# The low-part products of a flow-matching layer, moved behind the high-part products

## The chip, the cores and the metric

The kernel runs on one core of a Trainium2 chip. The metric is the device time of one execution in microseconds (us), as the median of several runs. Beside it there is a profile: one execution recorded by the hardware profiler.

## The reference, cut to what matters

One transformer-like layer is applied to 512 latent tokens and 128 context tokens, 640 in all, with a model width of 2048:

```python
h = _rmsnorm(x, norm1_g) * (1.0 + sc1) + sh1
p = h @ w_in                                  # 2048 x 5408
o_a, s_fin = _rwkv7_bidir(shift(p[..., :C_SHIFT]), s0, lp)
o_b = _chunk_gmlp(gelu(p[..., C_SHIFT:]), lp)
x = x + g1 * (concat([o_a, o_b]) @ w_out)     # 2048 x 2048
h = _rmsnorm(x, norm2_g) * (1.0 + sc2) + sh2
ff = (silu(h @ w_ffn_gate) * (h @ w_ffn_up)) @ w_ffn_down   # 2048 x 5632, 5632 x 2048
y = _rmsnorm(x + g2 * ff, final_norm_g)
```

The modulation vectors (`sh1`, `sc1`, ...) come from `silu(c) @ w_mod`. Everything is float32, and the large products have to keep nearly float32 accuracy.

## The kernel before, in words

**Split products.** TensorE multiplies in a faster, less exact format (fp32r). To keep the accuracy, each operand is split in two: `hi` is the value cast to fp32r, and `lo` is what the cast left over. A block of 128 x 128 weights and its activations then take three products into the same PSUM bank: `hi` weights by `hi` activations, `hi` weights by `lo` activations, and `lo` weights by `hi` activations. The fourth, `lo` by `lo`, is left out. A product here is one matmul of 128 x 128 weights with 320 columns (half of the tokens).

**Weight tiles.** Weights come in tiles of four such blocks (`[P, 4, P]`), in one transfer on the SyncE queue. For each tile ScalarE (ACT) casts `raw` to `hi`, then VectorE (DVE) subtracts `hi` from `raw` to make `lo`. In the FFN this is the helper `parts` (lines 1423 and 1424); for `w_in` and `w_out` it is `split` (lines 168 and 169). `raw`, `hi` and `lo` have three buffers each in the pool `st`, so the cast for a tile must wait until TensorE has read the `hi` of three tiles earlier, and the subtraction until it has read the `lo` of three tiles earlier.

**Stages.** In order of time:

- The modulation columns, the first norm and the product with `w_in`, block by block in `win` (lines 184 to 194): for each half of the tokens and each block `k`, the three products at lines 190, 191 and 192. After `k` = 1 and `k` = 3 the function `between` hands TensorE over to pieces of the RWKV preparation and the gMLP, which three queues of generators deal out.
- The RWKV recurrence, with the first half of the product with `w_out` dealt out between its hops.
- The second half of `w_out`: `four_blocks` (lines 1482 to 1484), one output block `m` after another, first for token half 0, then for half 1. `squares` squares each finished block on ACT and adds four of them up on GpSimd (POOL); `stats` (line 1462) sums over the partitions with a matmul by a matrix of ones. After the last group of a half it computes the norm factor `rs` with a DVE scaling, an ACT square root and a DVE reciprocal (lines 1465 to 1467). The normalised blocks of half 0 are made beside the blocks of half 1 (`first_half`, line 1392).
- The FFN. The first two output rows of gate and up are computed plainly (`plain`, lines 1571 to 1573). All others go through `seven` (lines 1642 to 1644), a Strassen-Winograd scheme with seven products where eight would be needed: 42 steps for gate and up (tiles of four blocks, two tiles a product) and 48 steps for the down projection (one tile a product). The 22 blocks of the down projection's inner dimension go in six chunks `CHK` = 3, 3, 4, 4, 4, 4, eight steps each; so in the first two chunks a tile has three blocks. Sums of weight tiles are made on POOL (`combined`, line 1552). The results of the products are taken from PSUM by hooks (`Gate`, `Sum` with lines 1876 to 1880, `Last`, `End`), written in the code some four products after the product itself. Near a change of chunk, new activation operands are split as well (`put_in`, lines 1708 on ACT and 1709 on DVE, three or four blocks at a time). In the last chunk, each PSUM bank is opened by a dummy matmul (line 2033) and filled with the sum so far by ACT (line 2034).

**What sets the order.** Each engine takes its instructions in a fixed order. On TensorE that order is the one written in the code in the set-up with the first three blocks of `w_in`, and in the recurrence (`manual_schedule`). In the other stages, and on the other engines, a planner that belongs to the framework arranges the instructions before the launch, by its own estimate of when each is ready, earlier code first. So the order on ACT, DVE and POOL isn't written out in the kernel and can come out another way when the program changes.

In a tile of `seven` the lines are these (`f` and `l` mark the first and the last product of a bank):

```python
for k in range(nk):
    xk = x(i, 4 * q + k)
    f, l = q == 0 and k == 0 and not filled, q == nq - 1 and k == nk - 1 and last
    TE.matmul(ps, hi[:, k, :], xk[:, 0, :], start=f, stop=False)
    TE.matmul(ps, hi[:, k, :], xk[:, 1, :], start=False, stop=False)
    TE.matmul(ps, lo[:, k, :], xk[:, 0, :], start=False, stop=l)
```

Of the kernel before, what the change touches and what calls it, by code (L numbers as in the profile page):

```python
# [21 lines left out]
KB = D // P  # L22
# [67 lines left out]
def flow_step(ctx: ExitStack, tc, x_prompt, x_sample, state_rwkv, c, c_ctx, w_mod, b_mod,  # L90
# [27 lines left out]
    for h in range(2):  # L118
        s = slice(CH * h, CH * h + CH)
# [64 lines left out]
    def win(halves, q, hi, lo, hfs=(0, 1), step=lambda k: None):  # L184

        for hf in hfs:
            s = slice(HALF * hf, HALF * hf + HALF)
            for k in range(4):
                kb = 4 * q + k
                TE.matmul(halves[hf], hi[:, k, :], h_hi[:, kb, s], start=(kb == 0), stop=False)  # L190
                TE.matmul(halves[hf], hi[:, k, :], h_lo[:, kb, s], start=False, stop=False)  # L191
                TE.matmul(halves[hf], lo[:, k, :], h_hi[:, kb, s], start=False, stop=(kb == KB - 1))  # L192
                wide[0] += 1
                step(k)

# [1165 lines left out]
    X = {}  # L1361
# [68 lines left out]
    with ExitStack() as ph:  # L1430
# [58 lines left out]
        for hf in range(2):  # L1489
            s = slice(HALF * hf, HALF * hf + HALF)  # L1490
            for m in range(KB):
                if hf or m >= AHEAD:
                    four_blocks(hf, m, 0)
                ps = four_blocks(hf, m, 1)
                if hf and m in (6, 7, 8, KB - 1):
                    for _ in range(2):
                        next(first)
                if sqs and (sqs[0][1] >= 12 or m % 4 == 1):
                    stats()
                add_out(m, [ps, ps], hf)  # L1500
                nc.sync.dma_start(d_x1[m][:, s], x1T[m][:, s])
                squares(hf, m)
                if hf and m > 1:
                    for kb in HALVES[m - 2:m - 1] if m < 14 else HALVES[2 * m - 16:2 * m - 14]:
                        first_half(kb)
                    if 4 <= m < 12:
                        j, i = divmod(m - 4, 2)
                        operand(1 + i, j, x1T[j + 8 * i][:, t1])
# [47 lines left out]
    def plain(e):  # L1556

        n, q, hs = PLAIN[e]
        for u in range(2):
            for b in range(2):  # L1560
                hi, lo = READY.pop(0) if READY else parts(PW.pop(0))
                next(loads, None)
                for h in hs:
                    if (n, u, h) not in CP:
                        CP[n, u, h] = pP.tile([P, 512], F32, tag="P", name="C")[:, 0:HALF]
                    ps, i = CP[n, u, h], ((1, 2), (5, 4))[h][b]
                    for k in range(4):
                        xk = X[i, 4 * q + k]
                        m = DONE.get((n, u, h), 0)
                        DONE[n, u, h] = m + 3  # L1570
                        TE.matmul(ps, hi[:, k, :], xk[:, 0, :], start=m == 0, stop=False)
                        TE.matmul(ps, hi[:, k, :], xk[:, 1, :], start=False, stop=False)
                        TE.matmul(ps, lo[:, k, :], xk[:, 0, :], start=False, stop=m == 45)

    def plain_out(n, h):

# [38 lines left out]
    def seven(b11, b12, b21, b22, x, hook, nk=4, bank=fresh, last=True, end=False):  # L1615

        def combine(out, a, b):
            combined(out, a, b, nk)
        t3 = [st.tile([P, 4, P], F32, tag="raw", name="t3", bufs=3) for _ in b11]
        combine(t3, b22, b12)  # L1620
        combine(b12, b12, b11)
        s6, s4 = b22, b21
        if end:
            s6, s4 = ([xap.tile([P, 4, P], F32, tag=next(wtags), name="rawd")] for _ in range(2))
            combine(s6, b22, b12)
            combine(s4, b21, s6)
        src = {1: b11, 2: b21, 3: b22, 7: t3, 5: b12, 6: s6, 4: s4}
        seq = PEND if end else PORD
        order = [raw for i in seq for raw in src[i]]

        ready = [parts(order.pop(0), nk)]
        for o, i in enumerate(seq):
            ps, filled = bank(i)
            nq = len(b11)
            for q in range(nq):
                hi, lo = ready.pop()
                if order:
                    ready.append(parts(order.pop(0), nk))
                for k in range(nk):
                    xk = x(i, 4 * q + k)  # L1640
                    f, l = q == 0 and k == 0 and not filled, q == nq - 1 and k == nk - 1 and last
                    TE.matmul(ps, hi[:, k, :], xk[:, 0, :], start=f, stop=False)  # L1642
                    TE.matmul(ps, hi[:, k, :], xk[:, 1, :], start=False, stop=False)  # L1643
                    TE.matmul(ps, lo[:, k, :], xk[:, 0, :], start=False, stop=l)  # L1644
            if i == 3 and not end:
                combine(b22, b22, b12)
                combine(b21, b21, b22)
            if last:
                hooks.append(lambda o=o, ps=ps: hook(o, ps))
            tick()  # L1650
            yield o
# [474 lines left out]
```

## Time and profile before

| | us |
|---|---|
| median of 3 runs | 3223.48 (3221.9 to 3225.47) |
| the profiled execution, its own time | 3213.3 |
| its span, first to last instruction | 3211.5 |
| TensorE busy by the page | 3088.0 (96%) |
| DVE busy | 2330.3 (73%) |
| ACT busy | 1460.1 (45%) |
| POOL busy | 1219.0 (38%) |

The profiled execution is one of its own, and 10.2 us below the median of the runs. The end of a matmul is modelled by the profiler and lies about 309 ns after its start, though the next one starts 147 ns after it; so "busy" on TensorE says that work was in flight, and a wait shows as idle only beyond those 309 ns. In the views, PE is TensorE's multiplying and PEld its loading of weights. A row of waits names who waited, for whom, and then microseconds in total, how many times, and the longest.

### The profile page before, as it was taken

The page shows a single profiled execution, that of the slowest core. Times are in us where ns is not written, and L with a number is a line of the kernel's source. Part 1 is how long each engine was busy: PE and PEld are TensorE (multiplying, and loading weights), DVE is VectorE, ACT ScalarE, POOL GpSimd, SP SyncE. Part 2 cuts the span into 40 slices and gives each one's busy share as a digit, 9 for nine tenths or more (in the row PEclk, how much of TensorE's full clock was granted, in tenths as well). Part 3 has the DMA queues.
Part 4 walks back from the last instruction along what each step waited for, and adds up shares of the span by engine and source line. Part 5 has one row for each costly group of instructions (what it writes and reads, how often), then busy time and mean ns, then how long its engine had stood idle before and what let it go on. Part 6 is the DMA issues. An engine that isn't in the chain of part 4 may idle for free.

```text
span 3211.5 us, 72260 instructions
## 1 busy us (share of the span) xinstructions
PE 3088.0 (96%) x28216; PEld 2858.2 (89%) x28216; DVE 2330.3 (73%) x4107; ACT 1460.1 (45%) x3197; POOL 1219.0 (38%) x1065
## 2 busy tenths in 40 slices
PE   6999989999999999999999999999999999999997
PEld 3688778788878888899999999999999999999997
DVE  4558666676657677767877777777777788887788
ACT  3344544454444444346644444444444454444365
POOL 2001121211122024311465566556655645555542
PEclk9999999999999999999999999999999999999999
DMA  9767786777778687564434434343344364553453
GB/s 372 239 187 203 210 215 171 209 218 193 201 198 216 210 275 253 173 200 133 141 116 130 127 105 123 118 124 118 113 128 126 104 199 152 159 165 112 140 165 122
DMA packets 740438, 550.88 MB, mean 172 GB/s; under 512 B 141056, under 2 KB 673504, under 8 KB 731264
## 3 DMA queue, kind: packets, MB, share of 16 engines
q1 hardware_dynamic: 727136, 532.47, 55.0%
q0 software_dynamic: 10624, 13.23, 1.9%
q8 instruction: 222, 3.64, 0.5%
q14 instruction: 120, 0.98, 0.1%
q10 hardware_dynamic: 2336, 0.57, 0.1%
HBM read 437.79 MB, written 110.95 MB: 171 GB/s over the span
## 4 chain that ended last, share of the span: by engine, by line
PE 56%; DVE 5%; issue 4%; DMA 3%; POOL 2%; ACT 2%; SPq 0%; DVEq 0%; POOLq 0%; ACTq 0%
PE P L1644 15%; PE P L1642 15%; PE P L1643 15%; DVE lo L1424 1%; PE big L1482 1%; PE big L1484 1%; PE big L1483 1%; PE big L1039 1%; PE big L190 1%; PE big L192 1%; PE big L191 1%; PE big L1041 1%; PE big L1040 1%; DMA opd<-d_op 1%; DMA rawd<-in_w_ffn_down_dram 1%
## 5 line engine op out<-in xcount | busy, mean ns | idle before, releaser
L1644 PE MATMUL P<-xo,lo 128*128 128x320 f32 x2352 | 727.1, 309 | 0.8 <-DVE lo L1424 0.7
L1642 PE MATMUL P<-xo,hi 128*128 128x320 f32 x2352 | 727.0, 309 | 0.7 <-ACT hi L1423 0.7
L1643 PE MATMUL P<-xo,hi 128*128 128x320 f32 x2352 | 726.9, 309 | 0.0
L1424 DVE TENSOR_TENSOR lo<-raw,hi 128x512 fp32r<-128x512 f32 x526 | 500.8, 955 | 174.4 <-ACT hi L1423 169.9
L1423 ACT CAST hi<-raw 128x512 fp32r<-128x512 f32 x526 | 326.7, 621 | 484.0 <-PE P L1643 392.1
L190 PE MATMUL big<-h_hi,hi 128*128 128x320 f32 x1376 | 447.3, 325 | 8.1 <-ACT hi L168 4.5
L1644 PEld LDWEIGHTS P<-xo,lo 128*128 128x128 f32 x2352 | 441.5, 188 | 1.8 <-DVE lo L1424 1.8
L1642 PEld LDWEIGHTS P<-xo,hi 128*128 128x128 f32 x2352 | 441.6, 188 | 1.0 <-ACT hi L1423 1.0
L1643 PEld LDWEIGHTS P<-xo,hi 128*128 128x128 f32 x2352 | 441.6, 188 | 0.0
L192 PE MATMUL big<-h_hi,lo 128*128 128x320 f32 x1376 | 431.1, 314 | 0.7 <-DVE lo L169 0.6
L191 PE MATMUL big<-h_lo,hi 128*128 128x320 f32 x1376 | 431.1, 313 | 0.7 <-DVE h_lo L352 0.4
L1552 POOL TENSOR_TENSOR raw<-raw 128x512 f32<-128x512 f32 x252 | 408.5, 1631 | 14.1 <-DVE lo L1424 2.7
L1644 PE MATMUL P<-xd,lo 128*128 128x320 f32 x1232 | 384.5, 312 | 16.3 <-DVE lo L1424 16.2
L1642 PE MATMUL P<-xd,hi 128*128 128x320 f32 x1232 | 382.7, 311 | 1.5 <-ACT hi L1423 0.3
L1643 PE MATMUL P<-xd,hi 128*128 128x320 f32 x1232 | 381.4, 310 | 0.0
L169 DVE TENSOR_TENSOR lo<-raw,hi 128x512 fp32r<-128x512 f32 x268 | 183.4, 689 | 200.6 <-ACT hi L168 185.1
L190 PEld LDWEIGHTS big<-h_hi,hi 128*128 128x128 f32 x1376 | 260.9, 190 | 58.1 <-issue 34.8
L1423 ACT CAST hi<-rawd 128x512 fp32r<-128x512 f32 (+1 forms) x288 | 168.8, 587 | 240.7 <-PE P L1643 203.1
L168 ACT CAST hi<-raw 128x512 fp32r<-128x512 f32 x268 | 164.5, 618 | 225.7 <-PE big L191 123.8
L191 PEld LDWEIGHTS big<-h_lo,hi 128*128 128x128 f32 x1376 | 261.3, 190 | 5.1 <-DVE h_lo L352 1.1
L192 PEld LDWEIGHTS big<-h_hi,lo 128*128 128x128 f32 x1376 | 260.3, 189 | 5.6 <-DVE lo L169 1.6
L1644 PEld LDWEIGHTS P<-xd,lo 128*128 128x128 f32 x1232 | 231.9, 188 | 23.2 <-DVE lo L1424 22.8
(404 smaller groups left out, 6052.8 us busy)
## 6 DMA issues: line engine op xcount, KB each, us to landing
wt<-in_w_mod_dram SPq DMA_DIRECT2D x96, 1024.0 KB
raw<-in_w_ffn_gate_dram SPq DMA_DIRECT2D x182, 256.0 KB
raw<-in_w_ffn_up_dram SPq DMA_DIRECT2D x182, 256.0 KB
rec<-d_S SPq DMA_DIRECT2D x80, 576.0 KB
raw<-in_w_in_dram SPq DMA_DIRECT2D x172, 256.0 KB
rawd<-in_w_ffn_down_dram SPq DMA_DIRECT2D x128, 256.0 KB
raw<-in_w_out_dram SPq DMA_DIRECT2D x96, 256.0 KB
xd<-d_os SPq DMA_DIRECT2D x66, 320.0 KB
```

Source lines behind the costliest of these rows:

```text
L168: S.copy(hi, raw)
L169: V.tensor_sub(lo, raw, hi.bitcast(F32))
L190: TE.matmul(halves[hf], hi[:, k, :], h_hi[:, kb, s], start=(kb == 0), stop=False)
L191: TE.matmul(halves[hf], hi[:, k, :], h_lo[:, kb, s], start=False, stop=False)
L192: TE.matmul(halves[hf], lo[:, k, :], h_hi[:, kb, s], start=False, stop=(kb == KB - 1))
L1039: TE.matmul(halves[hf], hi[:, k, :], o_hi[kb][:, s], start=(k == 0), stop=False)
L1423: S.copy(hi[:, 0:nk], raw[:, 0:nk])
L1424: V.tensor_sub(lo[:, 0:nk], raw[:, 0:nk], hi[:, 0:nk].bitcast(F32))
L1552: G.tensor_tensor(out=o[:, 0:nk], in0=p[:, 0:nk], in1=q[:, 0:nk], op=ALU.subtract)
L1642: TE.matmul(ps, hi[:, k, :], xk[:, 0, :], start=f, stop=False)
L1643: TE.matmul(ps, hi[:, k, :], xk[:, 1, :], start=False, stop=False)
L1644: TE.matmul(ps, lo[:, k, :], xk[:, 0, :], start=False, stop=l)
```

## The change

Three edits, all in the order of instructions; no instruction is added or taken out.

1. In `win`, the `lo` products of a pair of blocks follow the `hi` products of that pair: two `hi` products of block 0, two of block 1, then the two `lo` products. The hand-over to other work after `k` = 1 and `k` = 3 stays where it was.
2. In `plain` and `seven`, all `hi` products of a tile come first (eight for four blocks, six for three), then its `lo` products.
3. In the `w_out` stage, the sums of squares that `stats` takes at once, without waiting for an `m` with `m % 4 == 1`, are now only those of token half 1. The one it moves is the last group of half 0 (`m` = 12 to 15), which is summed after block 1 of half 1 where it was summed after block 0.

```diff
@@ win
                 TE.matmul(halves[hf], hi[:, k, :], h_hi[:, kb, s], start=(kb == 0), stop=False)
                 TE.matmul(halves[hf], hi[:, k, :], h_lo[:, kb, s], start=False, stop=False)
-                TE.matmul(halves[hf], lo[:, k, :], h_hi[:, kb, s], start=False, stop=(kb == KB - 1))
+                if k % 2:
+                    for j in (kb - 1, kb):
+                        TE.matmul(halves[hf], lo[:, j - 4 * q, :], h_hi[:, j, s], start=False, stop=(j == KB - 1))
@@ the w_out stage
-                if sqs and (sqs[0][1] >= 12 or m % 4 == 1):
+                if sqs and (sqs[0][0] and sqs[0][1] >= 12 or m % 4 == 1):
                     stats()
@@ plain
                         TE.matmul(ps, hi[:, k, :], xk[:, 0, :], start=m == 0, stop=False)
                         TE.matmul(ps, hi[:, k, :], xk[:, 1, :], start=False, stop=False)
-                        TE.matmul(ps, lo[:, k, :], xk[:, 0, :], start=False, stop=m == 45)
+                    for k in range(4):
+                        TE.matmul(ps, lo[:, k, :], X[i, 4 * q + k][:, 0, :], start=False,
+                                  stop=DONE[n, u, h] == 48 and k == 3)
@@ seven
                 for k in range(nk):
                     xk = x(i, 4 * q + k)
-                    f, l = q == 0 and k == 0 and not filled, q == nq - 1 and k == nk - 1 and last
-                    TE.matmul(ps, hi[:, k, :], xk[:, 0, :], start=f, stop=False)
+                    TE.matmul(ps, hi[:, k, :], xk[:, 0, :], start=q == 0 and k == 0 and not filled, stop=False)
                     TE.matmul(ps, hi[:, k, :], xk[:, 1, :], start=False, stop=False)
-                    TE.matmul(ps, lo[:, k, :], xk[:, 0, :], start=False, stop=l)
+                for k in range(nk):
+                    TE.matmul(ps, lo[:, k, :], x(i, 4 * q + k)[:, 0, :], start=False,
+                              stop=q == nq - 1 and k == nk - 1 and last)
```

## The prediction, made before the changed kernel ran

> **What bounds the kernel now.** I read the busy line of the page first, then the table of busy time by stretch over the stages that the change touches (its columns: length, then busy time and instructions of PE, PEld, DVE, ACT and POOL, then clock, DMA share, GB/s).
>
> ```profile
> PE 3088.0 (96%) x28216; PEld 2858.2 (89%) x28216; DVE 2330.3 (73%) x4107; ACT 1460.1 (45%) x3197; POOL 1219.0 (38%) x1065
> ```
> ```profile
> 200.00:1080.00 880.00, 844.27 (x10367) 713.59 (x10366) 592.83 (x1192) 414.40 (x899) 159.79 (x259) 0.99 0.73 199
> ...
> 1508.00:1575.00 67.00, 62.00 (x410) 60.16 (x411) 62.45 (x130) 49.02 (x113) 12.24 (x5) 1.00 0.48 139
> 1575.00:2580.00 1005.00, 1005.00 (x6854) 1005.00 (x6853) 762.98 (x959) 433.84 (x757) 612.61 (x412) 1.00 0.40 119
> 2580.00:2750.00 170.00, 164.72 (x1096) 161.99 (x1095) 137.28 (x229) 82.88 (x179) 85.34 (x74) 0.99 0.54 167
> 2750.00:3050.00 300.00, 293.34 (x1985) 290.88 (x1984) 239.15 (x352) 119.62 (x214) 159.22 (x106) 1.00 0.49 147
> ```
>
> TensorE is the bound. From 1575 to 2580, most of gate and up, it never stops: 1005 us by 6854 matmuls is 146.6 ns each. Nothing can be won there by order alone if the pitch doesn't depend on it, and the timeline of steady work says that it doesn't:
>
> ```profile
> 2400.23 0.31 PE L1642 MATMUL P<-xo,hi 128*128 128x320 f32 x1
> ...
> 2400.37 0.31 PE L1643 MATMUL P<-xo,hi 128*128 128x320 f32 x1
> ...
> 2400.52 0.31 PE L1644 MATMUL P<-xo,lo 128*128 128x320 f32 x1
> ...
> 2400.67 0.31 PE L1642 MATMUL P<-xo,hi 128*128 128x320 f32 x1
> ```
>
> Line 1643 uses the weights of 1642 and comes 0.14 after it; 1644 and the next 1642 bring new weights and come 0.15 after. So whether two products share weights or activations makes no difference, and as many weights are loaded as products made (x28216 twice in the busy line). What is left to win are waits. The waits by pair, for the whole span, name the one that the change is about:
>
> ```profile
> PE P L1644 <- DVE lo L1424: 16.9, 23, 1.5
> ...
> PE C L1573 <- DVE lo L1424: 3.1, 3, 1.7
> ...
> PE big L192 <- DVE lo L169: 0.6, 1, 0.6
> ```
>
> and asked for one stretch at a time, 2580 to 2750, 2750 to 3050 and 3050 to 3212, the first row splits so:
>
> ```profile
> PE P L1644 <- DVE lo L1424: 4.6, 5, 1.5
> ```
> ```profile
> PE P L1644 <- DVE lo L1424: 6.7, 8, 1.2
> ```
> ```profile
> PE P L1644 <- DVE lo L1424: 4.9, 8, 0.9
> ```
>
> (the other 2, of 0.7 in all, lie at 1569 and 1573). One such wait, in full:
>
> ```profile
> 2884.18 0.31 PE L1643 MATMUL P<-xd,hi 128*128 128x320 f32 x1
> 2885.64 0.41 PE L1644 MATMUL P<-xd,lo 128*128 128x320 f32 x1 [1.14 <-DVE lo L1424]
> 2885.89 0.30 PE L1642 MATMUL P<-xd,hi 128*128 128x320 f32 x1
> ```
>
> **Price of a wait.** 1644 starts 1.46 after 1643, not 0.147: 1.31 lost. That is the idle time shown, 1.14, and 0.162, because idle counts from a modelled end 0.309 after the start. And the product behind it comes after 0.25, not 0.147: 0.105 more. So a wait costs its row plus 0.267 us. All 23 cost 16.9 + 23 x 0.267 = 23.0 us, the 3 on line 1573 3.9, the one on 192 0.9.
>
> **Part 2 of the change, tiles in the FFN.** The same products at the same pitch: 0 for the work itself. The first `lo` product of a four-block tile comes third now and ninth after: its due time moves by 6 x 0.147 = 0.88 us, in a three-block tile by 4 x 0.147 = 0.59. A wait behind it shrinks by that, or goes with its restart. If tiles are late one behind the other, only the first wait gains: from the first `lo` of one tile to that of the next it is 12 products in either order.
>
> 2750 to 3050: of the eight, the timeline gives 1.05, 1.16, 0.42, 0.39, 1.14, 1.04, 0.39, 1.08 idle; the first and the last are quoted. The first falls in the last three-block tiles, as the DVE row of its subtraction shows (128x384):
>
> ```profile
> 2761.09 0.41 PE L1644 MATMUL P<-xd,lo 128*128 128x320 f32 x1 [1.05 <-DVE lo L1424]
> ```
> ```profile
> 2987.60 0.41 PE L1644 MATMUL P<-xd,lo 128*128 128x320 f32 x1 [1.08 <-DVE lo L1424]
> ```
> ```profile
> 2759.68 1.36 DVE L1424 TENSOR_TENSOR lo<-rawd,hi 128x384 fp32r<-128x384 f32 x1
> ```
>
> It gains 0.59. Four long ones gain 0.88 each and keep some 0.35; three short ones go, (0.40 + 0.267) each: 0.59 + 3.52 + 2.0 = 6.1.
>
> 3050 to 3212: eight waits, 4.9 + 8 x 0.267 = 7.0. The two longest are these:
>
> ```profile
> 3089.82 0.41 PE L1644 MATMUL P<-xd,lo 128*128 128x320 f32 x1 [0.78 <-DVE lo L1424]
> ```
> ```profile
> 3169.75 0.41 PE L1644 MATMUL P<-xd,lo 128*128 128x320 f32 x1 [0.89 <-DVE lo L1424]
> ```
>
> They gain 0.88, the six others go: 1.76 + (4.9 - 1.67) + 6 x 0.267 = 6.6.
>
> 2580 to 2750: five (1.14, 1.50, 0.40, 0.80, 0.75), all in three-block tiles. The first two:
>
> ```profile
> 2612.23 0.41 PE L1644 MATMUL P<-xd,lo 128*128 128x320 f32 x1 [1.14 <-DVE lo L1424]
> ...
> 2613.86 0.41 PE L1642 MATMUL P<-xd,hi 128*128 128x320 f32 x1 [0.34 <-ACT hi L1423]
> ...
> 2615.93 0.41 PE L1644 MATMUL P<-xd,lo 128*128 128x320 f32 x1 [1.50 <-DVE lo L1424]
> ```
>
> What the first gains is lost again at once to a late `hi`, which no reordering helps: 0. Then 0.59, 0.67 (gone), 0.59, 0.59: 2.4.
>
> 1508 to 1575, `plain`: DVE is busy 62.45 of 67, and its work isn't changed. The longest wait there is this one, and three more for `lo` and one for `hi` follow within 9 us:
>
> ```profile
> 1564.98 0.41 PE L1573 MATMUL C<-xo,lo 128*128 128x320 f32 x1 [1.68 <-DVE lo L1424]
> ```
>
>  Between 0 and 5.1 (the five there, 3.8 + 5 x 0.267); I take 1.0, the first wait's 0.88 and a restart.
>
> The last reader of a `hi` buffer comes 3 x 0.147 = 0.44 earlier in a tile, and casts wait for that:
>
> ```profile
> L1423 ACT CAST hi<-rawd 128x512 fp32r<-128x512 f32 x192 | 119.9, 624 | 179.3 <-PE P L1643 160.5 <-POOL rawd L1552 6.3 <-DVE acc L1880 5.0
> ```
>
> So a cast can start 0.44 earlier. I count this at 0: it can clear the four remainders of 0.35 + 0.267 (2.5 us won), or do nothing where ACT is held by something else, and below nothing it is the third rival. Against it stands how long the subtraction behind it can take:
>
> ```profile
> L1424 DVE TENSOR_TENSOR lo<-raw,hi x526: 676/693/1787, 1416.5 to 2602.1; 128x512 fp32r<-128x512 f32 x176
> ```
>
> 1787 where 693 is usual, while POOL works: 1.1 us more, of the size of the long waits. [...]
>
> New waits that take the place of old ones:
>
> ```profile
> PEld P L1642 <- ACT P L2034: 3.1, 8, 0.5
> ```
> ```profile
> PE P L1642 <- ACT hi L1423: 1.1, 2, 0.7
> ```
>
> Eight banks filled late by ACT in the last chunk, and two casts. With TensorE earlier each can grow, at most by what the `lo` waits beside them give, 6.6. They stand at the start of a product and are told off from TensorE's own transposes just ahead, so they move along; I take 1.0 off.
>
> The clock: one stretch after the waits at 2612 to 2616 ran slow.
>
> ```profile
> 2617.00:2621.00 4.00, 4.00 (x19) 4.00 (x18) 2.29 (x6) 1.70 (x4) 1.68 (x2) 0.57 0.86 250
> ```
>
> 19 matmuls where 4.0 / 0.147 = 27 fit: 1.2 us lost. Either it goes (1.2 won) or stays; I take 0, as two waits and the late `hi` stay. [...]
>
> **Part 1, pairs in `w_in`.** Products, pitch and hand-overs stay; the first `lo` of a pair is due 2 x 0.147 = 0.29 later. One wait of 0.6 + 0.267 gains 0.3. The planner may place the RWKV pieces beside them otherwise: TensorE is idle 880 - 844 = 36 us there, a tenth of it either way is 3.6; I take 0.
>
> **Part 3, the moved sum.**
>
> ```profile
> 1447.59 0.88 POOL L1452 TENSOR_TENSOR sumq<-sumq,sq 128x320 f32<-128x320 f32 x1 [2.65 <-ACT sq L1446]
> ```
> ```profile
> 1449.66 0.70 PE L1462 MATMUL ss<-sumq,ones 128*128 128x320 f32 x2
> ```
>
> The sum was ready at 1448.47, 1.2 before its matmul: there is no wait to remove. What moves are two matmuls, and behind them the norm factor and the blocks that need it, by 24 x 0.147 = 3.5 us. DVE has room for it before the stage ends:
>
> ```profile
> 1501.29 0.68 DVE L1052 SCALAR_TENSOR_TENSOR x1T<-big,modc,x1T 128x192 f32<-128x192 f32 x2 [3.38 <-PE big L1484]
> ...
> 1505.35 0.68 DVE L1052 SCALAR_TENSOR_TENSOR x1T<-big,modc,x1T 128x192 f32<-128x192 f32 x2 [3.38 <-PE big L1484]
> ```
>
> Twice 3.38 idle, for 3.5. So 0; if that cover is gone, up to 3.5 lost in `plain`, where DVE is full.
>
> **Sum.** 6.1 + 6.6 + 2.4 + 1.0 + 0.3 - 1.0 = 15.4 us. The profiled execution took 3213.3 (span 3211.5), so 3197.9 for it; the median of the runs shown is 10.2 higher, 3223.5 - 15.4 = **3208.1**.
>
> **Rivals.** *The wait moves on.* The `lo` waits go, but in the last chunk the ACT fills take all 6.6, as the late `hi` did at 2613.86, and `plain` gains nothing: 6.1 + 2.4 + 0.3 = 8.8, and half of the 6.1 and 2.4 lost to late casts where ACT sits behind a transfer: 4.6. That is 3218.9, no change that can be measured. For it: every long wait between 2750 and 3050 comes where operands are split, with ACT and DVE both late. Against stands the cast of the tile after the wait at 2885.64:
>
> ```profile
> 2883.23 0.62 ACT L1423 CAST hi<-rawd 128x512 fp32r<-128x512 f32 x1
> ```
>
> It ended at 2883.85, and with the wait cut to 0.35 its first product would be due some 4 x 0.147 after 2885.6, at 2886.2.
>
> *It doesn't do what it says.* For the sum of squares that is my forecast already (nothing waited). For `lo` it would need DVE to have been late by more than a tile; the waits show 1.7 at most.
>
> *DVE becomes the bound* (slower). An earlier cast puts the subtraction earlier at the head of DVE's queue, but its `lo` buffer is read until the end of the tile three back. DVE works in order: while the subtraction waits, the sums out of PSUM behind it wait too. At most 0.44 a tile. DVE has 300 - 239.15 = 60.85 spare over 1985 / 12 = 165 tiles, 0.37 each, so it decides from 0.37 of blocking on; at 0.44, 0.07 x 336 tiles of the down projection is 23.5 lost, with the gains there gone too (all but 1.3): 3245.7. Against it stands the order of today:
>
> ```profile
> 2852.85 0.62 ACT L1423 CAST hi<-rawd 128x512 fp32r<-128x512 f32 x1 [1.14 <-PE P L1643]
> ```
> ```profile
> 2852.99 0.49 DVE L1880 TENSOR_TENSOR acc<-acc,P 128x320 f32<-128x320 f32 x1 [0.56 <-PE P L1644]
> ```
>
> The cast would end at 2853.47 - 0.44 = 2853.03, and the tile's end was known at 2852.99: just late enough for no blocking.
>
> **How the numbers follow.** Forecast 0.72, the wait moves on 0.17, DVE the bound 0.11. The forecast's own range is 3194 to 3216: down to all waits and the slow clock gone (23.0 + 3.9 + 0.9 + 1.2 = 29.0, 3194.5), up to a gain of 8. For 8 in 10 the second case comes in and the third stays out: 3194 to 3225. A measurement of this kernel can tell about 0.2%, 6.4 us, from no change. The forecast is faster by more in all but 0.02 of its 0.72; a quarter of the second case, 0.04, lies beyond too; the third is slower: faster 0.74, same 0.15, slower 0.11.
>
> **What would show it.** Right: the row of waits for `lo` on the FFN's low-part line falls from 23 waits to six or seven short ones, and the steady stretch keeps 146.6 ns. The slower case: DVE's `lo` waiting for PE. The second: rows of PE waiting for ACT's `hi` or its fills that grow as the first falls. Wrong from the ground: a pitch other than 147 ns between two `lo` products, which the trace of before never has side by side; or waits in the stages before 1508 that change by more than the 3.6 allowed, which would say that the planner's order, not the due time, moved the time.

## The result, and the profile after

The changed kernel takes 3213.51 us (median of 10 runs, 3206.45 to 3220.7) against 3224.19 for the kernel before in as many runs beside it (3221.9 to 3227.8). The ratio is 0.9964, with a 95% interval of 0.9953 to 0.9974: 0.0036 x 3224.2 = 11.6 us faster. The forecast was 15.4. The profiled execution took 3210.43 us, its span is 3208.7.

The two profiled executions are only 2.9 us apart, because the one of the kernel before (3213.3) lies below all ten of its runs here. So the spans of two profiles are not compared below; waits, stage lengths and runs are.

These are waits by pair of the kernel after, over the whole span (TensorE waiting; total, times, longest):

```profile
PE P L1648 <- DVE lo L1426: 9.3, 12, 2.4
...
PE P L1645 <- ACT hi L1425: 3.1, 4, 1.9
...
PE big L190 <- ACT hi L168: 2.0, 4, 0.7
PE C L1576 <- DVE lo L1426: 1.9, 1, 1.9
...
PE pT L879 <- ACT M L873: 1.3, 2, 1.1
...
PE big L194 <- DVE lo L169: 0.3, 1, 0.3
```

Line 1648 is the old 1644, 1645 the old 1642, 1576 the old 1573, 879 the old 877 and 194 the old 192. The FFN's waits for `lo` fell from 16.9 us in 23 to 9.3 in 12. In the last chunk the row of line 2038 (a bank not yet emptied by DVE) and the fills of ACT (line 2039) come in. The same view for 2580 to 2750, 2750 to 3050 and 3050 to 3212:

```profile
PE P L1648 <- DVE lo L1426: 3.0, 4, 1.3
PE P L1645 <- ACT hi L1425: 2.9, 3, 1.9
PE P L1645 <- DVE acc L1883: 1.2, 1, 1.2
```
```profile
PE P L1648 <- DVE lo L1426: 1.7, 4, 0.7
```
```profile
PE P L2038 <- DVE cd L1920: 3.7, 4, 1.6
PE P L1645 <- ACT P L2039: 2.4, 2, 1.9
...
PE P L1648 <- DVE lo L1426: 1.2, 2, 0.9
```

Three different stories stand here. In the middle stretch the waits shrank and nothing replaced them. In the other two, other waits took their place. The table of busy time by stretch (columns as in the prediction) says the same by the count of matmuls:

```profile
1575.00:2580.00 1005.00, 1005.00 (x6838) 1005.00 (x6837) 757.44 (x958) 433.39 (x755) 624.47 (x409) 1.00 0.40 119
2580.00:2750.00 170.00, 162.85 (x1094) 160.24 (x1094) 136.07 (x231) 81.73 (x178) 82.12 (x71) 1.00 0.55 169
2750.00:3050.00 300.00, 298.22 (x2025) 296.64 (x2024) 237.06 (x359) 120.68 (x217) 161.75 (x109) 1.00 0.49 149
```

In the 300 us from 2750 TensorE does 2025 matmuls where it did 1985: 40 x 0.1466 = 5.9 us won. From 2580 to 2750 it does 1094 where it did 1096: nothing. The pitch of the steady stretch did not change, and a row of four `lo` products in it shows that they too come 0.147 apart ((0.75 - 0.31) / 3):

```profile
2400.59 0.75 PE L1648 MATMUL P<-xo,lo 128*128 128x320 f32 x4
```

Stage by stage, from the starts of the first matmuls of each in the trace (us). "Old" and "new" give the spread over all kernels here, those below too, that have the old order in that stage or the new one (or a variant of it, e5 and e6):

| stage | before | after | old | new |
|---|---|---|---|---|
| all of `w_in`, first to last product | 1029.9 | 1026.6 | 1029.6 to 1037.1 | 1026.0 to 1036.1 |
| first eighth of `w_in` | 126.6 | 125.9 | 126.4 to 128.0 | 124.3 to 126.4 |
| `plain` | 60.5 | 59.2 | 60.0 to 61.7 | 59.2 |
| first 168 products of `seven` | 26.9 | 32.0 | 26.9 to 30.2 | 29.2 to 32.0 |
| next 6720 products | 985.6 | 985.6 | 985.6 to 985.9 | 985.6 |
| down projection, chunk 0 | 80.5 | 79.1 | 79.9 to 81.3 | 78.3 to 79.9 |
| chunks 1 to 4 | 382.5 | 378.1 | 381.9 to 386.8 | 376.3 to 378.7 |
| last chunk | 125.0 | 124.9 | 124.4 to 125.4 | 123.3 to 127.3 |

Each kernel has one profile, so a row compares single executions; over the kernels all of `w_in` averages 1034.1 us with the old order and 1028.8 with the new. The stages between `w_in` and `plain`, not in the table, took 429.1 before and 431.5 after.

### The profile page after: what moved, and what is told of

Same layout as the page of the kernel before. It is cut to its first block, busy times and chain, and to the rows that moved or that the text cites. A ratio compares the mean times of both kernels' runs of the same rounds, so it can differ in the third digit from the quotient of the medians.

```text
span 3208.7 us, 72254 instructions
## 1 busy us (share of the span) xinstructions
PE 3091.3 (96%) x28216; PEld 2863.7 (89%) x28216; DVE 2321.3 (72%) x4107; ACT 1461.6 (46%) x3197; POOL 1223.0 (38%) x1065
## 4 chain that ended last, share of the span: by engine, by line
PE 58%; issue 5%; DVE 4%; DMA 2%; POOL 2%; ACT 1%; SPq 0%; DVEq 0%; POOLq 0%; ACTq 0%
PE P L1648 15%; PE P L1645 15%; PE P L1646 15%; PE big L190 1%; PE big L191 1%; PE big L194 1%; DVE lo L1426 1%; PE big L1484 1%; PE big L1485 1%; PE big L1486 1%; PE big L1041 1%; PE big L1043 1%; PE big L1042 1%; POOL ys L137 1%; DMA raw<-in_w_out_dram 0%
## 5 line engine op out<-in xcount | busy, mean ns | idle before, releaser
L1645 PE MATMUL P<-xo,hi 128*128 128x320 f32 x2352 | 700.5, 310 | 0.2 <-ACT hi L1425 0.2
L1646 PE MATMUL P<-xo,hi 128*128 128x320 f32 x2352 | 700.4, 310 | 0.0
L1648 PE MATMUL P<-xo,lo 128*128 128x320 f32 x2352 | 441.8, 310 | 4.1 <-DVE lo L1426 4.1
L190 PE MATMUL big<-h_hi,hi 128*128 128x320 f32 x1376 | 438.6, 325 | 5.1 <-ACT h_hi L353 2.9
L191 PE MATMUL big<-h_lo,hi 128*128 128x320 f32 x1376 | 423.5, 315 | 0.5 <-DVE h_lo L354 0.5
L1648 PEld LDWEIGHTS P<-xo,lo 128*128 128x128 f32 x2352 | 370.0, 188 | 4.9 <-DVE lo L1426 4.9
L1645 PE MATMUL P<-xd,hi 128*128 128x320 f32 x1232 | 367.8, 310 | 6.5 <-ACT hi L1425 2.9
L1646 PE MATMUL P<-xd,hi 128*128 128x320 f32 x1232 | 366.8, 309 | 0.0
L194 PE MATMUL big<-h_hi,lo 128*128 128x320 f32 x1376 | 324.1, 313 | 0.3 <-DVE lo L169 0.3
L1554 POOL TENSOR_TENSOR t<-raw 128x512 f32<-128x512 f32 x84 | 124.6, 1483 | 426.9 <-DMA raw<-in_w_ffn_up_dram 351.3
L1426 DVE TENSOR_TENSOR lo<-rawd,hi 128x512 fp32r<-128x512 f32 (+1 forms) x288 | 226.6, 794 | 25.2 <-ACT hi L1425 25.2
L1648 PE MATMUL P<-xd,lo 128*128 128x320 f32 x1232 | 236.9, 310 | 5.4 <-DVE lo L1426 5.2
```

Of the source, the lines that this page charges most:

```text
L194: TE.matmul(halves[hf], lo[:, j - 4 * q, :], h_hi[:, j, s], start=False, stop=(j == KB - 1))
L1426: V.tensor_sub(lo[:, 0:nk], raw[:, 0:nk], hi[:, 0:nk].bitcast(F32))
L1554: G.tensor_tensor(out=o[:, 0:nk], in0=p[:, 0:nk], in1=q[:, 0:nk], op=ALU.subtract)
L1645: TE.matmul(ps, hi[:, k, :], xk[:, 0, :], start=q == 0 and k == 0 and not filled, stop=False)
L1648: TE.matmul(ps, lo[:, k, :], x(i, 4 * q + k)[:, 0, :], start=False, stop=q == nq - 1 and k == nk - 1 and last)
```

## The experiments

**Theory A**, that of the prediction: what counts is when the first `lo` product of a tile is due; the gain sits in the FFN, and next to nothing in `w_in`. **Theory B**: the earlier release of `hi` is what gains. **Theory C**: neither; the planner deals the other engines' work anew once the order changes, and that gains or loses by chance. Every ratio is to the kernel before on the same chip, with its 95% interval; its median was 3223.29 us beside e1 to e4, 3226.14 beside e5 to e8 and 3224.42 beside e9 to e12.

### The parts alone

**e1**, the FFN's order alone; **e2**, the pairs of `w_in` alone; **e3**, the moved sum alone. Each is one of the hunks of the diff shown above:

```diff
@@ e1: plain and seven            (w_in and the sums as before)
+                for k in range(nk):
+                    TE.matmul(ps, lo[:, k, :], x(i, 4 * q + k)[:, 0, :], start=False, ...
@@ e2: win                        (the rest as before)
+                if k % 2:
+                    for j in (kb - 1, kb):
@@ e3: the w_out stage            (the rest as before)
+                if sqs and (sqs[0][0] and sqs[0][1] >= 12 or m % 4 == 1):
```

> The kernel before with the change in the FFN alone (plain and seven). Theory A, the due time: the low part is due 0.88 us later and waits shrink, so nearly the whole change is here: 9 to 15 us faster than before, a ratio of 0.995 to 0.997, and the waits of TensorE for lo between 2750 and 3212 fall from 11.6 us to under 4. Theory B, the planner's new order did it and the due time is incidental: the ratio lies anywhere between 0.995 and 1.003, and the waits for lo fall only where DVE's order was changed.

> The kernel before with the pairs in w_in alone. Theory A: 0.3 us, not to be told from no change (0.999 to 1.001), and the end of the w_in stage at 1079 us within 1 us. Theory B: the planner deals the RWKV pieces out anew, and the end of the w_in stage moves by some 3 us, as it did in the changed kernel (1075 for 1079), with waits of TensorE for other tiles than lo changed on both sides.

> The kernel before with the moved sum of squares alone. Theory A: 0 (0.999 to 1.001), since the sum was ready 1.2 us before its matmul. Theory B: a new order of DVE and ACT behind 1450 us, and up to 3.5 us lost in plain, or as much won.

Measured: e1 3216.84 us, 0.9985 (0.997 to 1.0); e2 3216.63 us, 0.9979 (0.9966 to 0.9991); e3 3226.83 us, 1.0002 (0.9992 to 1.0013). The sum of the three is -0.34%, the whole change -0.36%: the parts add up. But they stand the wrong way round for theory A: the FFN, forecast at 15.1 us, gave 0.0015 x 3223 = 4.8 (0 to 9.7 by the interval), and `w_in`, forecast at 0.3, gave 6.8 (2.9 to 11.0). The moved sum gave nothing, as forecast. In e1 the waits for `lo` from 2750 to 3212 did fall below the 4 us expected, to 1.7 in four; but waits for banks and fills, 2.7 in five and 3.6 in two, came in there. The profiled execution of e2, at 3222.59 us the third longest of its twelve, shows no gain in `w_in` (1036.1 us).

### Is it the order at all, and which half of it?

**e4** exchanges the two `hi` products of each block in `seven` and leaves due times and releases alone. **e5** puts the `lo` products late but the last `hi` product behind them, so `hi` is released last. **e6** leaves the first `lo` product third and releases `hi` earlier. As lists of (weights, block, activations), 0 for high and 1 for low:

```diff
-  for k: (0, k, 0) (0, k, 1) (1, k, 0)
+  e4  for k: (0, k, 1) (0, k, 0) (1, k, 0)
+  e5  all (0, k, 0) (0, k, 1) but the very last; all (1, k, 0); then the last (0, k, 1)
+  e6  (0, 0, 0) (0, 0, 1) (1, 0, 0); (0, k, 0) (0, k, 1) for the other k; (1, k, 0) for them
```

> A control: in seven the two hi products of each block change places (hi weights by lo activations first, then by hi activations, then lo weights), so the low part's due time and the release of the buffers stay where they were. Theory A: no change (0.999 to 1.001), the 23 waits for lo stay. Theory B: the planner comes to another order anyway and the time moves by more than 0.2% either way.

> In seven alone: all hi products but the last, then the lo products, then the last hi product. The low part is due eighth instead of third (0.73 us later for four blocks), but the hi buffer is released last of all, 0.15 us later than before. Theory A, the due time: the waits for lo in the five chunks before the last shrink as in the kernel with the whole FFN edit, and chunks 0 to 4 together take some 6 us less than before. Theory B, the early release of hi (casts 0.44 us earlier) is what counts: chunks 0 to 4 stay within 2 us of before.

> In seven alone: the first block's three products as before (its lo third), then the hi products of the other blocks, then their lo products. The low part is due third as before, the hi buffer is released two products earlier (0.29 us). Theory A: the waits for lo stay, 23 of 16.9 us or so, and chunks 0 to 4 stay within 2 us of before. Theory B: chunks 0 to 4 take 4 us less or more.

Measured: e4 3224.2 us, 1.0004 (0.9991 to 1.0017); e5 3217.61 us, 0.9981 (0.9972 to 0.999); e6 3220.75 us, 0.9982 (0.9973 to 0.9991). The control e4 is even. In the down projection none of ACT's 606 instructions stands elsewhere in its order, and at most one of DVE's 730; in e1, e5 and e6 some 100 to 110 of ACT's and 145 to 170 of DVE's do. So theory C isn't tested apart from the other two by e5 and e6. In total time these can't be told apart, and by the chunks e5 met the expectation of theory A and e6 that of theory B: chunks 0 to 4 took 463.0 us before and 462.9 in e4, but 457.1 in e5 and 458.2 in e6. The waits of TensorE for `lo` from 2580 to 3070 differ: 11.3 us in 13 before, 9.3 in 13 in e4, 8.7 in 13 in e6, but 4.8 in 7 in e5. So the later due time removes such waits, and the earlier release leaves as many, a little shorter. In e6's chunks all waits together are worth 3.1 us less than before (8.5 in 14 for 11.6 in 14), and a piece of slow clock that cost the kernel before 1.7 us is missing.

The clock bears on the total times too. In the 82 runs of the kernel before beside e1 to e12, 0.001 of mean granted clock goes with 2.1 us. The runs of e6 were granted 0.0015 more than those of the kernel before beside them: some 3 of the 5.8 us between the two means. For e5 it is 0.0004, some 1 of 7.5, and for e2 0.0019, some 4 of 5.9. Less the clock, then, e5 gains more than e6, which speaks for the due time, and the gain of e2 is smaller than it looks. What went ahead of such pieces in the traces is told at the end.

### What the start of the FFN and the last chunk give back

**e7** is the changed kernel with `plain` left in the old order.

```diff
@@ e7: plain
-                    for k in range(4):
-                        TE.matmul(ps, lo[:, k, :], X[i, 4 * q + k][:, 0, :], start=False,
-                                  stop=DONE[n, u, h] == 48 and k == 3)
+                        TE.matmul(ps, lo[:, k, :], xk[:, 0, :], start=False, stop=m == 45)
```

> The changed kernel with plain left as it was before. In the profile of the changed kernel the first 168 products of seven took 5 us more than before: a long wait for a lo at 1574 and a slow clock behind it. Theory A, plain's order brings TensorE to that lo too early: here the stretch from the start of plain to product 168 of seven is back within 1 us of before (87.4 us), and the whole is 2 to 4 us faster than the changed kernel. Theory B, seven's own order does it through the planner's order on DVE: the wait and the slow clock stay, and the whole is within 1 us of the changed kernel or slower.

Measured: 3212.14 us, 0.9959 (0.9947 to 0.9971), even with the changed kernel. `plain` takes 60.5 again, but the start of `seven` still takes 29.2 us, and the last chunk 123.3. So the order in `plain` is not what makes the start slow.

**e9** has the new order only in chunks 1 to 4 of the down projection; **e10** adds the order by tile in `w_in` (e8, below).

```diff
@@ e9: seven, with behind = 0 < c < NC - 1 in the down projection, else False
-                    TE.matmul(ps, lo[:, k, :], xk[:, 0, :], start=False, stop=l)
+                    if not behind:
+                        TE.matmul(ps, lo[:, k, :], xk[:, 0, :], start=False, stop=l)
+                for k in range(nk * behind):
+                    TE.matmul(ps, lo[:, k, :], x(i, 4 * q + k)[:, 0, :], start=False, ...
```

> The FFN's new order only in chunks 1 to 4 of the down projection; gate and up, chunk 0, the last chunk and everything else as before. If the chunks won what their waits for the low parts cost, and the start of the FFN and the last chunk gave it back because of the new order there: the first 168 products of seven take 26.9 us as before, chunks 1 to 4 again 362 to 365 us against 382 before, and the whole is 5 to 8 us faster (0.9975 to 0.9985), more than with the order in the whole FFN (0.9985). If instead the last chunk takes 125 us anyway and the chunks before it gain only what they then lose in it: within 0.1% of the kernel before, and the last chunk over 125 us.

> The same, and in w_in the low parts of all four blocks behind the eight high products. If the two gains add up, 0.9945 to 0.9957 (-0.31% for w_in by tile, -0.15 to -0.25% for the chunks). If the gain in w_in belongs to the one arrangement of the planner that a change there alone gives, and not to the order of the products, it is as e9 within 0.1%.

(The 362 to 365 us in the first of them is a slip of addition: the four chunks of e1 add up to 377.2.) Measured: e9 3216.29 us, 0.9967 (0.9954 to 0.998); e10 3206.76 us, 0.9937 (0.9922 to 0.9953), **the fastest of all**, 17.7 us below the kernel before. Chunks 1 to 4 took 378.6 and 376.3. No gain of the order elsewhere in the FFN can be seen: with it in these chunks alone, the gain is not less than that of the whole FFN (0.9967 and 0.9985, with overlapping intervals). The gains of e8 (0.31%, below) and e9 (0.33%) add up to that of e10 (0.63%, five runs). Two things were not as expected: e9's gain lies above the 5 to 8 us named (its interval reaches into them), and the start of `seven` took 30.2 us in it although its order is the old one. The timeline of e9 there:

```profile
1580.39 0.41 PE L1645 MATMUL P<-xo,lo 128*128 128x320 f32 x1 [1.88 <-DVE lo L1424]
...
1582.75 0.63 PE L1645 MATMUL P<-xo,lo 128*128 128x320 f32 x1 [0.41 <-DVE lo L1424]
```

A `lo` 1.88 late, then the slow clock (0.53 granted from 1581.5 to 1585.1, matmuls of 0.63 where 0.31 is usual). What differs from the kernel before is to be seen on POOL and DVE, first before, then in e9:

```profile
1572.13 4.08 POOL L1758 TENSOR_TENSOR s<-act 128x320 f32<-128x320 f32 x1 [6.06 <-DVE xo L1382]
1572.77 0.69 DVE L1424 TENSOR_TENSOR lo<-raw,hi 128x512 fp32r<-128x512 f32 x1
```
```profile
1577.67 1.06 POOL L1762 TENSOR_TENSOR s<-act 128x320 f32<-128x320 f32 x1 [6.06 <-DVE xo L1382]
1578.99 1.35 DVE L1424 TENSOR_TENSOR lo<-raw,hi 128x512 fp32r<-128x512 f32 x1
```

The instructions and their order are the same. In one execution POOL's sum takes 4.08 us and the `lo` beside it 0.69, in the other POOL's sum takes 1.06 and the `lo` 1.35. All fourteen profiles go by this: in the six where that sum takes 4.08 the stretch takes 26.9 us, in the eight where it takes 1.05 or 1.06 it takes 29.2 to 32.0. Of the nine kernels with the old order there six are of the first kind and three of the second; all five with the new one or a variant of it are of the second. So it isn't the order alone that decides it.

What stops the last chunk is to be seen in the changed kernel from 3080 to 3088, first TensorE, then ACT, then DVE:

```profile
3087.16 0.41 PE L1645 MATMUL P<-xd,hi 128*128 128x320 f32 x1 [1.92 <-ACT P L2039]
```
```profile
3085.83 0.43 ACT L1914 COPY tp<-P 128x320 f32<-128x320 f32 x1 [3.94 <-DVE cd L1931]
...
3086.67 0.43 ACT L2039 COPY P<-acc 128x320 f32<-128x320 f32 x1
```
```profile
3082.30 1.58 DVE L1926 TENSOR_TENSOR cd<-cd,tp 128x320 f32<-128x320 f32 x1
3083.81 1.58 DVE L1904 SCALAR_TENSOR_TENSOR cd<-cd,modc,x1d 128x320 f32<-128x320 f32 x1
3085.32 0.48 DVE L1931 TENSOR_TENSOR cd<-P,tp 128x320 f32<-128x320 f32 x1
```

Read it backwards. TensorE waits for a fill of ACT; the fill stands on ACT behind a copy that waits 3.94 us for DVE's evacuation at 3085.32 (a sum that empties a bank); and that evacuation stands on DVE behind two instructions of 1.58. Before the change these two (old lines 1921 and 1899) took 0.48 and 1.07, while the `lo` between them took 1.78:

```profile
3083.53 1.07 DVE L1899 SCALAR_TENSOR_TENSOR cd<-cd,modc,x1d 128x320 f32<-128x320 f32 x1
3084.52 1.78 DVE L1424 TENSOR_TENSOR lo<-rawd,hi 128x512 fp32r<-128x512 f32 x1
3086.23 0.48 DVE L1921 TENSOR_TENSOR cd<-cd,tp 128x320 f32<-128x320 f32 x1
```

In the changed kernel POOL sums weight tiles from 3077.32 to 3086.52 without a break; before, the instruction of 0.48 began in a gap of 0.63 us between two such sums. So DVE's slow instructions moved from one place to another, and its work in the chunk stayed as it was (104.75 us busy in 125 before, 105.43 after).

The four waits of the row of line 2038 (1.62, 0.74, 0.38 and 0.97) begin elsewhere. DVE's rows ahead of the longest, and TensorE's:

```profile
3108.52 0.55 DVE L1904 SCALAR_TENSOR_TENSOR cd<-cd,modc,x1d 128x320 f32<-128x320 f32 x1 [2.82 <-DMA x1d<-d_x]
3108.99 1.28 DVE L1426 TENSOR_TENSOR lo<-rawd,hi 128x512 fp32r<-128x512 f32 x2
3110.19 0.48 DVE L1920 TENSOR_TENSOR cd<-P,cd 128x320 f32<-128x320 f32 x1
```
```profile
3110.73 0.42 PE L2038 MATMUL P<-xd 128*128 128x320 f32 x1 [1.62 <-DVE cd L1920]
```

DVE stood idle for the transfer of `x1d`, the residual to which the next two output blocks are added; the code asks for it only with the last sum of the two blocks before (`load_x1`). Two `lo` and the evacuation came behind it, and TensorE waited for that. All four are of this kind (DVE waited 1.57 to 2.82 for `x1d` ahead of them). Before the change DVE had the same order and waited for `x1d` as well, 9.9 us in seven waits against 13.5 in seven now, but TensorE never waited for that evacuation (old line 1915). So with the waits for `lo` gone, TensorE reaches what stands behind this transfer. Whether asking for `x1d` earlier gives the 3.7 us back is untested.

### Where `w_in` gains

**e8** puts the four `lo` products of a `w_in` tile behind all eight `hi` products. **e11** does that, but with the tile's last `hi` product behind the `lo` products; **e12** leaves block 0 as before and puts only the `lo` products of blocks 1 to 3 behind.

```diff
@@ e8: win
-                TE.matmul(halves[hf], lo[:, k, :], h_hi[:, kb, s], start=False, stop=(kb == KB - 1))
+                if k == 3:
+                    for j in range(4 * q, 4 * q + 4):
+                        TE.matmul(halves[hf], lo[:, j - 4 * q, :], h_hi[:, j, s], start=False, stop=(j == KB - 1))
@@ e11: the h_lo product of k == 3 goes behind that loop
@@ e12: in place of the loop
+                for j in {0: (0,), 3: (1, 2, 3)}.get(k, ()):
+                    TE.matmul(halves[hf], lo[:, j, :], h_hi[:, 4 * q + j, s], start=False, ...
```

> w_in alone, by tiles of four blocks as in the FFN: eight hi products, then four lo products; other work still comes after block 1 and after block 3, so after four and after eight products of a tile half instead of six and six. Theory A, w_in gained by the due time or the earlier release of hi: as fast as the pairs or faster (0.998 or less). Theory B, w_in gained by how the planner dealt the RWKV pieces out anew: another deal, anything between 0.996 and 1.006, and the waits for the pieces' tiles, not for lo, make the difference.

> w_in alone: the first low product of a tile is due 8th of 12 as with the order by tile (which gave 0.9969) but the high part is read last of all, so it is released one product later than before. By the theory that the later due time is what gains: 0.9965 to 0.9975. By the theory that the earlier release of the high part does it (the next cast starts sooner): 1.000, or slightly over. If only the planner's new arrangement counts, a gain of any size, and DVE's idle-ending share of 15 us in that stage changes as well.

> w_in alone: block 0 as before, so the first low product is due 3rd as before, then the high products of blocks 1 to 3 and their low products, so the high part is released two products (0.29 us) sooner. By the theory of the earlier release: 0.997 to 0.998. By the theory of the due time: 0.9995 to 1.0005. If both this and e11 gain about the same, neither is the cause by itself, and what they have in common is a new arrangement of the other engines.

Measured: e8 3215.83 us, 0.9969 (0.9957 to 0.9981); e11 3218.83 us, 0.9974 (0.9962 to 0.9987); e12 3220.72 us, 0.9988 (0.9975 to 1.0002). That looks as if the later due time gained and the earlier release did not. But the intervals of e11 and e12 overlap, and e11's runs were granted 0.0018 more clock than those of the kernel before beside them, e12's 0.0002: some 4 of the 6.5 us between the means of e11, next to nothing of the 3.6 of e12. Less the clock the two gain alike, and so it is in their profiles: all of `w_in` takes 1028.4 us in e11 and 1036.8 in e12, and slow clock costs 17.1 and 25.6 of it. So the total times don't decide between due time and release in `w_in`. The waits are asked too, from 50 to 1080, in this order: before, e11, e12.

```profile
PE pT L877 <- ACT M L871: 4.6, 4, 3.4
PE big L190 <- ACT hi L168: 4.5, 3, 2.0
...
PE pmm L519 <- DVE zv L698: 1.7, 1, 1.7
...
PE big L192 <- DVE lo L169: 0.6, 1, 0.6
```
```profile
PE pmm L523 <- DVE zv L702: 4.6, 3, 2.9
...
PE big L190 <- ACT hi L168: 1.7, 4, 0.6
PE pT L881 <- ACT M L875: 1.5, 3, 1.0
```
```profile
PE big L190 <- ACT hi L168: 4.5, 3, 2.8
PE pmm L520 <- DVE zv L699: 4.0, 2, 3.5
...
PE pT L878 <- ACT M L872: 2.8, 2, 2.6
...
PE big L193 <- DVE lo L169: 0.8, 2, 0.6
```

The row for `lo` was always small. What went are waits for ACT, three of them above all: at 75 and 99 us for a cast (1.96 and 2.04 before) and at 476 for the copy `M` (3.41). The last is there in all eight kernels in which the first `lo` of a `w_in` tile is due third (2.08 to 3.41), and in none of the six in which it is due later. But waits for DVE's `zv` came in, and all idle time of TensorE in `w_in` fell by less than these three: from 46.0 us in 71 waits before to 42.8 in 64 in e11 (44.8 in 66 in e12), and over the kernels from 46.7 with the old order to 43.1 with the new. How the wait at 476 went is to be seen in the kernel before, ACT and then DVE:

```profile
474.27 0.74 ACT L711 ACTIVATE gq<-gq 128x640 f32<-128x640 f32 x1 [5.58 <-DVE gq L709]
...
475.34 0.86 ACT L871 COPY M<-pM 32x320 f32<-32x320 f32 x2
```
```profile
471.69 0.19 DVE L802 COPY mx<-mix 80x30 f32<-80x30 f32 x1 [2.75 <-DMA mix<-dd]
471.82 0.69 DVE L169 TENSOR_TENSOR lo<-raw,hi 128x512 fp32r<-128x512 f32 x1
...
473.42 0.82 DVE L709 TENSOR_TENSOR gq<-gq,praw 128x640 f32<-128x640 f32 x1
```

and in e11:

```profile
470.28 0.74 ACT L715 ACTIVATE gq<-gq 128x640 f32<-128x640 f32 x1 [1.78 <-DVE gq L713]
```
```profile
467.24 0.68 DVE L169 TENSOR_TENSOR lo<-raw,hi 128x512 fp32r<-128x512 f32 x1
...
469.34 0.20 DVE L806 COPY mx<-mix 80x30 f32<-80x30 f32 x1 [0.69 <-DMA mix<-dd]
469.44 0.81 DVE L713 TENSOR_TENSOR gq<-gq,praw 128x640 f32<-128x640 f32 x1
```

Before, DVE waited 2.75 us for a transfer that the copy `mx` needs; then came a `lo` and three other pieces, and only then, 1.73 us after the copy, the multiplication that makes `gq`. ACT waited 5.58 us for it, and the copy `M` that TensorE needed stood behind it in ACT's order. In e11 a `lo` comes ahead of the copy, and `gq` right behind it, 0.10 us after. All eight kernels whose first `lo` is due third have the first order (1.73), all six others the second (0.10 at most). So for this wait theory A's cause and theory C's way go together: the due time decides, but through the planner's order on DVE and ACT and not through a wait for `lo`. The `lo` itself is only 0.61 of the 1.73; the rest of the 5.58 is other pieces and the transfer, for which DVE waited 0.7 to 1.9 us in the other kernels. The waits at 75 and 99 lie in the set-up, whose order on TensorE is written out; they fell to 0.6 or less with the order by tile, but with the pairs they are 1.98 and 1.41 in e2, 1.62 and 1.32 in e7, and 0.64 and 0.73 in the changed kernel. That the wait for `lo` behind them (0.6) holds up the chain of modulation product, DVE and ACT is argued and not shown. Nor is it shown that these three waits are the whole gain: with the order unchanged `w_in` took between 1029.6 and 1037.1 us, slow clock included.

## Why the prediction was right, and where it was not

The time lies in the range and the direction is right, by a sum whose terms were partly wrong and made up for one another; that part is luck. The sign it named for being right came only in part: the pitch held, but the row of waits for `lo` fell to 12 of 9.3 us, the longest 2.4, and not to six or seven short ones.

- **Price and pitch** held: steady work keeps its pitch, `lo` after `lo` too.
- **2750 to 3050, -6.1**: right in mechanism and size. The `lo` waits went from 6.7 in eight to 1.7 in four: 5.0 + 4 x 0.267 = 6.1, and 40 more matmuls fit, 5.9 us. Over the kernels chunks 1 to 4 average 384.3 with the old order and 377.7 with the new. (In the two profiles shown they differ by 4.4, for chunk 1 got no shorter.) The four that remain were forecast at some 0.35 each and are 0.43 on average; by the prediction's own rows only 0.16 to 0.28 of the long ones would have been left.
- **2580 to 2750, -2.4**: the `lo` waits shrank by 1.6, but late casts (2.9, where 0.3 had been) and a late sum of DVE (1.2) came in their place: 0 in this window. Chunk 0 itself gained 1.4 us, here and over the kernels (old 80.5, new 79.1 on average); here that is about what the slow clock had cost (1.7 us).
- **3050 to 3212, -6.6 with 1.0 off for new waits**: the step that failed. The `lo` waits gave 3.7 + 6 x 0.267 = 5.3 us where 6.6 was forecast, but the term for new waits was sized 1.0 and measured 5.9 (3.7 + 2.4, less the 0.2 of before; with 0.267 for each of the five waits more, 7.2). Nothing was left, 125.0 to 124.9; the balance of some 2 us lies in waits too short for a row, ahead of a product's first `hi`. The rival "the wait moves on" was right that nothing would be left here, but the fills it named took only 2.2; the 3.7 are banks that DVE had not emptied, which it did not name. I had taken the rows of the fills to mean that they move along with TensorE; they stood behind DVE, and DVE behind its slow instructions and the transfer of `x1d`.
- **The start of `seven`** was given no term. It lost 5.1 us in this execution and 2.3 on average (27.9 to 30.2): it is long where POOL's sum there took 1.05 or 1.06 us (29.2 to 32.0) and short where that took 4.08 (26.9).
- **`plain`, -1.0**: right in size (60.5 to 59.2), and nothing of it can be seen in the time (e7).
- **`w_in`, -0.3 with the planner's 3.6 either way taken as 0**: wrong. It gave 6.8 us (2.9 to 11.0 by the interval of e2), and by tiles 10.0, some 4 of it in each case with a higher granted clock. I had priced the row of `lo` waits and not the order that the planner gives DVE and ACT around it. The prediction's own sign for this, waits before 1508 that change by more than 3.6, came: the two rows for ACT fell from 9.1 to 3.3 us, and TensorE's idle time in `w_in` from 46.0 to 38.7.
- **The moved sum, 0**: right. **DVE the bound**: not so; new waits of TensorE for it came in the last chunk and once in chunk 0 (1.2).
- **The slow clock at 2617, 0**: it went in this profile, but another came at 1574. By the granted clock of its row it had cost 0.43 x 4 = 1.7 us, not 1.2.

The FFN's sum was thus 15.1 and the FFN gave 4.8 (0 to 9.7); `w_in` made up for 6.5 of the difference.

## What to carry to other kernels

Moving the late operand's products behind the others was worth about its price where the engine that makes it has nothing else due just behind, as in chunks 1 to 4; where it has, as in the last chunk, the wait only changes its name, so look in that engine's queue for what it delivers next, and for what that queue itself waits for. The same reordering can pay where no wait names the operand, because a planner then gives the other engines another order; the rows of waits don't tell how much. Apply such an order stage by stage and keep it where its stage shortens: that gave the fastest kernel here.

## What the runs showed of the hardware

**The clock fell behind stretches with idle time.** The table rows around the two places, before the change and after it (first the stretch with the waits, then the one behind; the third column from the end is the granted clock):

```profile
2613.00:2617.00 4.00, 2.15 (x13) 1.63 (x12) 4.00 (x7) 2.10 (x5) 1.98 (x2) 1.00 0.51 182
```
```profile
1570.00:1574.00 4.00, 1.66 (x9) 1.36 (x9) 4.00 (x7) 2.97 (x8) 2.39 (x3) 0.94 0.34 107
1574.00:1581.00 7.00, 6.83 (x27) 6.83 (x28) 6.03 (x8) 2.41 (x5) 4.48 (x4) 0.55 0.20 61
```

After 1.85 us of idleness in 4 the matmuls from 2617 came at a clock of 0.57 (the row in the prediction); after 2.34 in 4, those from 1574 came at 0.55: 27 in 7.0 us, where 7.0 / 0.147 = 48 fit. At the lower clock of 0.50 (granted from 1575 to 1578) the slow part of the 4 us from 2617 is 0.43 x 4 / 0.5 = 3.4 us. The longest single waits were 1.50 (behind 1.14 and 0.34) and 2.43 (behind 1.08 and 0.21); in the second place the slow piece began at 1573.52, within the wait.

In the records of the granted clock each of these two profiles ends in a slow piece of some 16 us that the end cuts off. The 19 ahead of these two (9 before the change, 10 after) were all granted 0.50; 12 lasted 3.41 us, six 6.83 and one 10.24, and within an execution their starts lie whole multiples of 3.41 us apart. Cut into stretches of 3.41 us along these starts, from the first product of `w_in` to the end of the FFN, the two profiles show this: of the 15 full-clock stretches in which TensorE was busy (by the modelled ends) for less than half, 12 were followed by a slow one; of the 35 with a half to 0.7, 3; of the 1768 with more, none. So all 15 drops there came behind a stretch in which the idle time, summed, was 30% or more, while 35 such stretches had none behind them. Of the slow pieces, 3.41 us cost 1.7 where TensorE has work. Why they come and go from one execution to the next was not shown.

**DVE beside POOL.** A DVE sum of two SBUF operands took 0.48 us in one place and 1.58 in another (lines 1921 and 1926, the same instruction): 0.48 where it began in the gap of 0.63 us between two sums of POOL, 1.58 while POOL summed from 3077.32 to 3086.52. At the start of `seven` POOL's sum took 4.08 where DVE's `lo` took 0.69, and 1.06 where it took 1.35. What makes the one or the other slow was not shown. What the change moved in the last chunk was which instruction is slow, not how much: DVE was busy 104.75 us of 125 before and 105.43 after.
